# Attention of a hybrid decoder trunk: one stream of score visits in place of one schedule per head pair

## The chip, the cores and the metric

The kernel runs on one core of a Trainium2 chip. The metric is the device time of one execution in microseconds (us). TensorE (PE in the rows) multiplies matrices, VectorE (DVE) and ScalarE (ACT) work on elements, GpSimd (POOL) and SyncE (SP) issue transfers. Each of them has its own queue of instructions.

## The reference, cut to what matters

Layer 0 of the trunk is differential attention over 512 positions and 16 heads, layer 1 a chunked spatial gating MLP. Each head has two score maps; the second one's probabilities are weighted by lambda and subtracted from the first's.

```python
def probs(qq, kk):
    s = jnp.einsum('bhqd,bhkd->bhqk', qq, kk).astype(jnp.float32) * scale + bias
    s = jnp.where(causal, s, -jnp.inf)
    return jax.nn.softmax(s, axis=-1)
a = probs(q_i[0], k1) - lam * probs(q_i[1], k2)
return jnp.einsum('bhqk,bhkd->bhqd', a.astype(v.dtype), v)
...
o = rms_norm(o, subln_g) * (1.0 - lam_init)
```

The outputs of the heads are gated, multiplied by the output projection and added to the residual stream.

## The kernel before, in words

Products are done in halves of a number: every weight and every activation is split into a high and a low part (`hi`, `lo`: one copy on ScalarE, one subtraction on VectorE), and three matmuls of 512 columns stand for one product. A chunk of weights is loaded by SyncE into `raw` tiles and split in four pieces, which `Chunk.tick` spreads over the matmuls of the chunk before it.

Attention is the stage from 203 to 517 us of the trace. Its work comes in these steps:

- `project_qk(p)` makes the queries and keys of head pair p: 32 units, each of three matmuls (L254 to L256), with two chunks of weights split beside them. The results are read out of PSUM by ScalarE (`qkh`, L504) and VectorE (`qkl`, L505).
- A `Group` is a visit: one or two blocks of 128 queries, of one head or of both heads of a pair, side by side in tiles of 512 columns. The causal mask leaves block i with (i + 1) x 128 keys. A pair has five groups: (one, 3); (one, 2) and (one, 0); (one, 1) and (two, 1); (two, 3); (two, 2) and (two, 0).
- `Group.scores` issues 6 or 12 matmuls (L694); VectorE adds the bias and finds the maximum (L704), ScalarE takes exponentials and their sums (L707), two or four of each; VectorE then divides and subtracts the second map (L711 to L715). The result is `e`.
- `Group.flip` transposes `e` on TensorE (`pa`, L721), and ScalarE copies it out (`at`, L723).
- `Group.values` multiplies it by the values (`po`, L732). The last one of a head calls `Head.normalise`: four squares with sums on ScalarE (L662), eleven small VectorE instructions for the root (L180 to L192), and a product `on` (L666).
- `Head.close` transposes `on` on TensorE (`pto`, L672), and VectorE gates it into `yT` (L673).

`attention_steps` lays the five groups of one pair out in ten slots: scores in slots 0 to 4, the flip of group t in slot t + 2, its values in slot t + 3, the close of head one in slot 6 and that of head two in slot 9. `interleave` runs a slot and then as many units of the filler as keep it even over the ten slots: 3 or 4. The filler is `project_qk` of the next pair, 32 units; pairs 7 and 8 share the last projection and 48 units of the output projection (`out_half`, L273 to L275), 40 units each. At the end of a pair the filler is drained, and the next pair begins with slot 0. So scores are issued in the first half of a pair, and none in the second half.

The order in the code is a priority, not the order of the queues: a planner that reckons with times of its own lays out the queue of each engine when the kernel is built. A step whose inputs aren't ready by its reckoning lets later ones pass. On the chip each queue then runs in the order laid out. The eight banks of PSUM come from one pool, taken in turn by whatever step asks.

Of the kernel before, what the change touches and what calls it, by code (L numbers as in the profile page):

```python
# [10 lines left out]
F32 = mybir.dt.float32  # L11
F32R = mybir.dt.float32r
# [4 lines left out]
P = 128  # L17
D = 1024
S = 512
BR = 2048  # L20
NH = 16
HALF = 64
NB = S // P
# [27 lines left out]
def build(ctx, tc, x, rel_bias, attn_norm, w_in, lq1, lk1, lq2, lk2, subln, w_out,  # L51
# [14 lines left out]
    def bank(name):  # L66
        return psum.tile([P, S], F32, tag="ps", name=name)
# [102 lines left out]
    make_identity(nc, ident)  # L170
    flip = const.tile([P, P], F32, name="flip")
    nc.vector.tensor_copy(flip, ident[:, ::-1])

    MAGIC = 1597463007.0 - 2.0 ** 22 - 2.0 ** 30
# [14 lines left out]
    def rsqrt(dst, ssum, n, scale):  # L189

        v = small.tile([P, n], F32, name=f"rv{n}")
        nc.vector.tensor_scalar(v, ssum, -0.5 * scale, -0.5 * EPS, ALU.mult, ALU.add)  # L192
        newton(dst, v, n)
# [56 lines left out]
    def proj_t(ps, w, c):  # L250

        cs = slice(c * P, (c + 1) * P)
        for k in range(KD):
            nc.tensor.matmul(ps, lhsT=w.hi[:, k, cs], rhs=hT[0][:, k, :], start=(k == 0), stop=False)  # L254
            nc.tensor.matmul(ps, lhsT=w.hi[:, k, cs], rhs=hT[1][:, k, :], start=False, stop=False)  # L255
            nc.tensor.matmul(ps, lhsT=w.lo[:, k, cs], rhs=hT[0][:, k, :], start=False, stop=(k == KD - 1))  # L256
            w.tick()
            yield

    def out_half(i0, m, store, cs=range(4), acc=None, finish=None):  # L260

        for c in cs:
            w = Chunk(i0 + c, 16)
            yh, yl = store(c)
            for i in range(4):
                k = 4 * c + i
                nc.scalar.copy(yh[:, i], yT[:, k, :])  # L267
                nc.vector.tensor_tensor(yl[:, i], yT[:, k, :], yh[:, i].bitcast(F32), ALU.subtract)  # L268
            for b in range(NB):
                bs = slice(b * P, (b + 1) * P)  # L270
                for j in range(4):
                    k = 4 * c + j
                    nc.tensor.matmul(acc[b], lhsT=yh[:, j, bs], rhs=w.hi[:, j, :], start=(k == 0), stop=False)  # L273
                    nc.tensor.matmul(acc[b], lhsT=yh[:, j, bs], rhs=w.lo[:, j, :], start=False, stop=False)  # L274
                    nc.tensor.matmul(acc[b], lhsT=yl[:, j, bs], rhs=w.hi[:, j, :], start=False, stop=(k == KB - 1))  # L275
                    w.tick()
                    yield
                if c == 3:
                    finish(b)

    def run(g):
        for _ in g:
            pass
# [17 lines left out]
    def product_n(ps, a, w, start):  # L301

        more = {} if start else {"skip_group_check": True}
        for i in range(2):
            rs = slice(i * P, (i + 1) * P)
            for k in range(4):
                nc.tensor.matmul(ps[i], lhsT=a[0][:, k, rs], rhs=w[0][:, k, :], start=(start and k == 0), stop=False, **more)
                nc.tensor.matmul(ps[i], lhsT=a[0][:, k, rs], rhs=w[1][:, k, :], start=False, stop=False, **more)
                last_mm[:] = [nc.tensor.matmul(ps[i], lhsT=a[1][:, k, rs], rhs=w[0][:, k, :], start=False,
                                               stop=(k == 3), **more)]  # L310
                yield
# [98 lines left out]
    def residual(r, m, acc):  # L410
        def finish(b):
            ms = slice(m * S, (m + 1) * S)
            add = nc.vector.tensor_tensor(xr[:, b, ms], acc[b], xr[:, b, ms], ALU.add)
            square(r, b, m)
            if m == 0:
                half_mean(r, b)
            return add
        return finish
# [72 lines left out]
    def project_qk(p):  # L491
        qk = []
        for which in range(2):
            w = Chunk(qk_at[p] + which, 16)
            for j in range(2):
                ps = bank("psqk")
                yield from proj_t(ps, w, j)
                th = att.tile([P, NB, P], F32R, tag="qkh", name="qkh", bufs=6)
                tl = att.tile([P, NB, P], F32R, tag="qkl", name="qkl", bufs=6)
                sc = HALF ** -0.5 if which == 0 else 1.0  # L500
                pr = ps.rearrange("p (b n) -> p b n", b=NB)
                if which == 0:
                    pr = pr[:, :, ::-1]
                nc.scalar.activation(th, pr, AF.Copy, scale=sc)  # L504
                nc.vector.scalar_tensor_tensor(tl, pr, sc, th.bitcast(F32), ALU.mult, ALU.subtract)  # L505
                qk.append((th, tl))
        QK[p] = qk
# [49 lines left out]
    for c in range(2):  # L557
        pt = bank("pt")
        sl = slice(c * (TLEN // 2), (c + 1) * (TLEN // 2))
# [71 lines left out]
    att = scope.__enter__()  # L631

    def fetch_values(g):
        V[g] = att.tile([P, 4, NB, P], F32, name="v")
        nc.gpsimd.dma_start(V[g].rearrange("p j b n -> p (j b n)"), vd[g])

    fetch_values(0)
    run(project_qk(0))

    nc.scalar.activation(le, ls, AF.Exp)  # L640
# [3 lines left out]
    class Head:  # L644
# [12 lines left out]

        def normalise(self):
            ssq = small.tile([P, NB], F32, name="ssq")
            self.on = att.tile([P, NB, P], F32, name="on", bufs=1)  # L660
            for ii in range(NB):
                nc.scalar.activation(self.on[:, ii, :], self.po[:, ii * P:(ii + 1) * P], AF.Square,  # L662
                                     accum_out=ssq[:, ii:ii + 1])
            rs = small.tile([P, NB], F32, name="rso")
            rsqrt(rs, ssq, NB, 1.0 / P)
            nc.vector.tensor_tensor(self.on, self.po.rearrange("p (b n) -> p b n", b=NB),  # L666
                                    rs.unsqueeze(2).broadcast_to([P, NB, P]), ALU.mult)
# [7 lines left out]
    class Group:  # L675
# [42 lines left out]
        def flip(self):  # L718
            pa = bank("pa")
            for c in range(0, self.width, P):  # L720
                nc.tensor.transpose(pa[:, c:c + P], self.e[0][:, c:c + P], ident)  # L721
            self.at = att.tile([P, S], F32, name="at", bufs=2)
            nc.scalar.copy(self.at[:, 0:self.width], pa[:, 0:self.width])  # L723

        def values(self):
# [9 lines left out]
                if hd.left == 0:  # L735
                    hd.normalise()

    def attention_steps(heads):

        one, two = heads  # L740
        groups = [Group((one, 3)), Group((one, 2), (one, 0)), Group((one, 1), (two, 1)), Group((two, 3)),
                  Group((two, 2), (two, 0))]
        slots = [[] for _ in range(len(groups) + 5)]
        for t, g in enumerate(groups):
            slots[t].append((2, g.scores))
            slots[t + 2].append((0, g.flip))
            slots[t + 3].append((1, g.values))
        slots[6].append((3, one.close))
        slots[9].append((3, two.close))
        return [[f for _, f in sorted(sl, key=lambda z: z[0])] for sl in slots]  # L750

    def interleave(slots, filler, units, drain=True):
        n = len(slots)
        done = 0
        for t, sl in enumerate(slots):
            for f in sl:
                f()
            want = units * (t + 1) // n
            while done < want:
                if next(filler, StopIteration) is StopIteration:  # L760
                    break
                done += 1
        if drain:
            run(filler)

    i0 = out_at
    acc = {}

    def last_units():
        yield from project_qk(NH // 2 - 1)  # L770
        for b in range(NB):
            acc[b] = bank(f"acc{b}")
        yield from out_half(i0, 0, hT_store, range(3), acc)

    rest = last_units()
    for p in range(1, NH // 2 + 1):
        steps = attention_steps([Head(2 * p - 2), Head(2 * p - 1)])
        if p % 2 and p < NH // 2 - 1:
            fetch_values(p // 2 + 1)
        if p < NH // 2 - 1:  # L780
            interleave(steps, project_qk(p), 32)
        else:
            interleave(steps, rest, 40, p == NH // 2)
    scope.__exit__(None, None, None)
    quarters = tc.tile_pool(name="quarters", bufs=1)
    qp = quarters.__enter__()
# [120 lines left out]
    for n in range(BR // D):  # L907
        for i in range(7):
# [7 lines left out]
            units = product_n(ps, a, w, i in (0, 1, 3))  # L916
# [48 lines left out]
    for b in range(NB):  # L965
        sl = slice(b * P, (b + 1) * P)
# [31 lines left out]
    for m in range(2):  # L998
        for gates in (True, False):
            n = VB + 2 * m + (not gates)  # L1000
# [49 lines left out]
    last = residual(2, 1, acc)  # L1050
# [41 lines left out]
```

## Time and profile before

| what | us |
|---|---|
| median of 3 runs (lowest, highest) | 935.14 (934.59, 936.24) |
| the profiled execution, its own time | 936.22 |
| its span, first to last instruction | 934.5 |
| TensorE busy in the span | 898.9 |
| VectorE busy | 649.0 |
| ScalarE busy | 474.5 |

The profile is of one execution. Its own time is 1.1 us over the median, and 1.7 us of it lie outside the span. Busy times of TensorE are modelled at their ends: a matmul of 512 columns shows some 390 ns, but the next one starts about 230 ns after it.

### The profile page before, as it was taken

How to read it: one execution, taken by the hardware profiler on the slowest of the kernel's cores; microseconds unless marked ns; L12 is line 12 of the kernel's file. 1: busy time of each engine (PE TensorE's matmuls, PEld its weight loads, DVE VectorE, ACT ScalarE, POOL GpSimd, SP SyncE). 2: the span in 40 equal slices, each digit the busy share in tenths (PEclk: the TensorE clock that was granted, in tenths of full speed). 3: DMA queues.
4: the chain of work that ended last, by engine and by line, in shares of the span. 5: the costliest groups of instructions: out<-in, count | busy, mean ns of one | idle time of the engine just before them, and what ended most of it. 6: DMA issues, size and time to landing. Idle time of an engine off the chain costs nothing.

```text
span 934.5 us, 14107 instructions
## 1 busy us (share of the span) xinstructions
PE 898.9 (96%) x5393; PEld 772.1 (83%) x5393; DVE 649.0 (69%) x1399; ACT 474.5 (51%) x1015; POOL 34.3 (4%) x52
## 2 busy tenths in 40 slices
PE   7999999999999999999999999999999999999996
PEld 5778999977777777777777887778899999998885
DVE  6936575367767777677778937885978777776634
ACT  7635465356446454464556614663645444455432
POOL 0000100000000000000000001100100000000000
PEclk9999999999999999999999999999999999999999
DMA  8547745552132223122212604456455654534202
GB/s 291 214 103 214 202 159 113 183 183 82 61 102 63 87 77 103 57 66 91 71 45 88 249 24 110 135 139 195 106 172 125 193 135 137 114 112 139 90 21 90
DMA packets 55828, 115.48 MB, mean 124 GB/s; under 512 B 3965, under 2 KB 20398, under 8 KB 52432
## 3 DMA queue, kind: packets, MB, share of 16 engines
q1 hardware_dynamic: 49120, 79.70, 25.3%
q0 software_dynamic: 5584, 33.56, 15.0%
q10 hardware_dynamic: 1056, 1.32, 0.4%
q8 instruction: 42, 0.69, 0.3%
q14 instruction: 26, 0.21, 0.1%
HBM read 89.36 MB, written 6.33 MB: 102 GB/s over the span
## 4 chain that ended last, share of the span: by engine, by line
PE 62%; DVE 23%; ACT 8%; DMA 4%; issue 3%; SPq 0%; ACTq 0%; POOLq 0%; DVEq 0%
PE px L319 15%; PE py L319 11%; PE acc L273 5%; PE acc L274 5%; PE acc L275 5%; ACT e L707 5%; DVE lo L130 4%; PE psv L480 3%; DMA quarter<-quarter 3%; DVE e L715 3%; PE psqk L254 2%; PE psqk L255 2%; PE psqk L256 2%; DVE e L704 2%; DVE e L714 2%
## 5 line engine op out<-in xcount | busy, mean ns | idle before, releaser
L374 DVE TENSOR_TENSOR lo<-quarter,hi 128x1024 fp32r<-128x1024 f32 x126 | 152.7, 1234 | 87.3 <-ACT hi L373 86.9
L373 ACT CAST hi<-quarter 128x1024 fp32r<-128x1024 f32 x126 | 128.8, 1047 | 125.9 <-DMA quarter<-quarter 40.8
L130 DVE TENSOR_TENSOR lo<-raw,hi 128x512 fp32r<-128x512 f32 x144 | 94.2, 684 | 37.4 <-ACT hi L129 37.2
L129 ACT CAST hi<-raw 128x512 fp32r<-128x512 f32 x144 | 81.5, 621 | 67.2 <-PE psqk L255 37.1
L254 PE MATMUL psqk<-hT,hi 128*128 128x512 f32 x256 | 107.1, 418 | 0.0
L707 ACT ACTIVATE e<-e,nm 128x384 f32<-128x384 f32 (+3 forms) x128 | 70.6, 553 | 67.7 <-DVE nm L704 67.6
L256 PE MATMUL psqk<-hT,lo 128*128 128x512 f32 x256 | 101.9, 398 | 0.0
L255 PE MATMUL psqk<-hT,hi 128*128 128x512 f32 x256 | 101.1, 395 | 0.0
L319 PE MATMUL py<-hT,hi 128*128 128x256 f32 x512 | 93.0, 283 | 0.0
L273 PE MATMUL acc<-hi,hT 128*128 128x512 f32 x224 | 88.1, 393 | 0.0
L275 PE MATMUL acc<-hi,hT 128*128 128x512 f32 x224 | 87.4, 390 | 0.0
L274 PE MATMUL acc<-lo,hT 128*128 128x512 f32 x224 | 87.3, 390 | 0.0
L319 PEld LDWEIGHTS py<-hT,hi 128*128 128x128 f32 x512 | 79.7, 192 | 0.0
L319 PE MATMUL py<-hT,lo 128*128 128x256 f32 x256 | 72.4, 283 | 0.0
L254 PEld LDWEIGHTS psqk<-hT,hi 128*128 128x128 f32 x256 | 49.0, 191 | 15.4 <-issue 5.1
L704 DVE CUSTOM_DVE_ANT_0 e<-pss,bias 128x384 f32<-128x384 f32 (+3 forms) x128 | 55.6, 484 | 3.0 <-PE pss L694 2.9
L256 PEld LDWEIGHTS psqk<-hT,lo 128*128 128x128 f32 x256 | 48.7, 190 | 10.8
L255 PEld LDWEIGHTS psqk<-hT,hi 128*128 128x128 f32 x256 | 49.0, 191 | 8.7
L268 DVE TENSOR_TENSOR hT<-yT,hT 128x512 fp32r<-128x512 f32 x56 | 37.4, 688 | 25.6 <-PE acc L274 17.2
L267 ACT CAST hT<-yT 128x512 fp32r<-128x512 f32 x56 | 33.1, 621 | 38.0 <-PE acc L274 28.0
L273 PEld LDWEIGHTS acc<-hi,hT 128*128 128x128 f32 x224 | 42.1, 188 | 9.4 <-issue 0.7
L275 PEld LDWEIGHTS acc<-hi,hT 128*128 128x128 f32 x224 | 42.1, 188 | 9.0
(218 smaller groups left out, 2033.4 us busy)
## 6 DMA issues: line engine op xcount, KB each, us to landing
quarter<-in_sgu_w_in SPq DMA_DIRECT2D x48, 512.0 KB, 5.0
raw<-in_attn_w_in SPq DMA_DIRECT2D x38, 512.0 KB, 4.5
quarter<-quarter POOLq DMA_DIRECT2D x18, 1024.0 KB, 7.2
quarter<-in_attn_w_in SPq DMA_DIRECT2D x24, 512.0 KB, 4.8
raw<-in_attn_w_out SPq DMA_DIRECT2D x16, 512.0 KB, 4.3
raw<-in_sgu_w_out SPq DMA_DIRECT2D x16, 512.0 KB, 4.2
vd<-yT POOLq DMA_DIRECT2D x4, 1024.0 KB, 6.0
v<-vd POOLq DMA_DIRECT2D x4, 1024.0 KB, 5.0
```

The source lines that it names most:

```text
L129: nc.scalar.copy(hi[:, sl], raw)
L130: nc.vector.tensor_tensor(lo[:, sl], raw, hi[:, sl].bitcast(F32), ALU.subtract)
L254: nc.tensor.matmul(ps, lhsT=w.hi[:, k, cs], rhs=hT[0][:, k, :], start=(k == 0), stop=False)
L255: nc.tensor.matmul(ps, lhsT=w.hi[:, k, cs], rhs=hT[1][:, k, :], start=False, stop=False)
L256: nc.tensor.matmul(ps, lhsT=w.lo[:, k, cs], rhs=hT[0][:, k, :], start=False, stop=(k == KD - 1))
L273: nc.tensor.matmul(acc[b], lhsT=yh[:, j, bs], rhs=w.hi[:, j, :], start=(k == 0), stop=False)
L274: nc.tensor.matmul(acc[b], lhsT=yh[:, j, bs], rhs=w.lo[:, j, :], start=False, stop=False)
L275: nc.tensor.matmul(acc[b], lhsT=yl[:, j, bs], rhs=w.hi[:, j, :], start=False, stop=(k == KB - 1))
L319: nc.tensor.matmul(ps[f // 2][:, f % 2 * H:(f % 2 + 1) * H], lhsT=w[x][:, k, f * P:(f + 1) * P], rhs=a[y][:, k, :], start=clear, stop=(k = ...
L373: nc.scalar.copy(hi[:, sl], raw[:, sl])
L374: nc.vector.tensor_tensor(lo[:, sl], raw[:, sl], hi[:, sl].bitcast(F32), ALU.subtract)
L707: nc.scalar.activation(e[f][:, cs], e[f][:, cs], AF.Exp, scale=-1.0, bias=nm[:, col], accum_out=l[:, col])
```

## The change: what it does

The five visits of all eight pairs become one line of 40. Slot s issues the scores of visit s first, then two units of filler, the flip of visit s - 2, two more units, the values of the same visit, one unit, a close if one is due, and the rest of the units. A pair has five slots with 6 or 7 units each instead of ten with 3 or 4. Head one is closed in the first slot of the next pair and head two in its third, each one slot after its last values. The last pair has the 48 units of the output projection as filler and four more slots. Four kinds of tiles get more buffers: `qkh` and `qkl` 8 for 6, `on` 2 for 1, `at` 3 for 2.

```diff
-                th = att.tile([P, NB, P], F32R, tag="qkh", name="qkh", bufs=6)
-                tl = att.tile([P, NB, P], F32R, tag="qkl", name="qkl", bufs=6)
+                th = att.tile([P, NB, P], F32R, tag="qkh", name="qkh", bufs=8)
+                tl = att.tile([P, NB, P], F32R, tag="qkl", name="qkl", bufs=8)
...
-            self.on = att.tile([P, NB, P], F32, name="on", bufs=1)
+            self.on = att.tile([P, NB, P], F32, name="on", bufs=2)
...
-            self.at = att.tile([P, S], F32, name="at", bufs=2)
+            self.at = att.tile([P, S], F32, name="at", bufs=3)
...
-    def attention_steps(heads):
...
-        slots = [[] for _ in range(len(groups) + 5)]
-        for t, g in enumerate(groups):
-            slots[t].append((2, g.scores))
-            slots[t + 2].append((0, g.flip))
-            slots[t + 3].append((1, g.values))
-        slots[6].append((3, one.close))
-        slots[9].append((3, two.close))
-        return [[f for _, f in sorted(sl, key=lambda z: z[0])] for sl in slots]
-
-    def interleave(slots, filler, units, drain=True):
-        n = len(slots)
-        done = 0
-        for t, sl in enumerate(slots):
-            for f in sl:
-                f()
-            want = units * (t + 1) // n
-            while done < want:
...
-    def last_units():
-        yield from project_qk(NH // 2 - 1)
+    def out_units():
         for b in range(NB):
             acc[b] = bank(f"acc{b}")
         yield from out_half(i0, 0, hT_store, range(3), acc)
 
-    rest = last_units()
-    for p in range(1, NH // 2 + 1):
-        steps = attention_steps([Head(2 * p - 2), Head(2 * p - 1)])
-        if p % 2 and p < NH // 2 - 1:
-            fetch_values(p // 2 + 1)
-        if p < NH // 2 - 1:
-            interleave(steps, project_qk(p), 32)
-        else:
-            interleave(steps, rest, 40, p == NH // 2)
+    PAIRS, VISITS, LAG = NH // 2, 5, 2
+    line, heads = [], {}
+
+    def visits(p):
+        one, two = (Head(2 * p + i) for i in range(2))
+        heads[p] = one, two
+        return [Group((one, 3)), Group((one, 2), (one, 0)), Group((one, 1), (two, 1)), Group((two, 3)),
+                Group((two, 2), (two, 0))]
+
+    def slot(s, filler, units):
+
+        todo = []
+        if s < PAIRS * VISITS:
+            if s % VISITS == 0:
+                line.extend(visits(s // VISITS))
+            todo.append((0, line[s].scores))
+        if 0 <= s - LAG < len(line):
+            todo.append((2, line[s - LAG].flip))
+            todo.append((4, line[s - LAG].values))
+        for i, ready in enumerate((2, 4)):
+            p, r = divmod(s - LAG - ready - 1, VISITS)
+            if r == 0 and 0 <= p < PAIRS:
+                todo.append((5, heads[p][i].close))
+        done = 0
+        for at, f in todo:
+            while done < min(at, units) and next(filler, StopIteration) is not StopIteration:
+                done += 1
+            f()
+        while done < units and next(filler, StopIteration) is not StopIteration:
+            done += 1
+
+    tail = out_units()
+    for p in range(PAIRS):
+        if p % 2 == 0 and p < PAIRS - 2:
+            fetch_values(p // 2 + 1)
+        last = p == PAIRS - 1
+        filler = tail if last else project_qk(p + 1)
+        for r in range(VISITS + (LAG + 2 if last else 0)):
+            slot(p * VISITS + r, filler, 6 + (r in (1, 3)))
+        run(filler)
```

## Rows read from the trace of the kernel before

**Rows 1.** The page's first part: busy us, share of the span, instructions.

```profile
PE 898.9 (96%) x5393; PEld 772.1 (83%) x5393; DVE 649.0 (69%) x1399; ACT 474.5 (51%) x1015; POOL 34.3 (4%) x52
```

**Rows 2.** Busy time by stretch (PE, PEld, DVE, ACT, POOL; PEclk): attention, one pair of it.

```profile
203.20:517.50 314.30, 297.96 (x1733) 238.62 (x1732) 232.24 (x783) 170.50 (x537) 8.61 (x16) 0.99 0.24 76
241.40:280.90 39.50, 37.33 (x213) 29.85 (x212) 27.98 (x96) 20.03 (x66) 1.61 (x3) 0.96 0.29 94
```

**Rows 3.** Who waited for whom, 203.2 to 517.5 us: total, times, longest.

```profile
DVE r L711 <- ACT e L707: 34.9, 32, 1.3
...
DVE lo L130 <- ACT hi L129: 16.0, 7, 4.1
PE pto L672 <- DVE on L666: 13.9, 12, 2.1
DVE rv L192 <- ACT on L662: 11.1, 8, 1.7
DVE yT L673 <- PE pto L672: 10.3, 14, 1.0
...
PE pa L721 <- DVE e L715: 2.1, 6, 1.0
```

**Rows 4.** TensorE in order of time, the close of a head one.

```profile
262.07 1.06 PE L732 MATMUL po<-v,at 128*128 128x128 f32 x8
262.89 0.48 PE L254 MATMUL psqk<-hT,hi 128*128 128x512 f32 x1
...
268.22 0.39 PE L256 MATMUL psqk<-hT,lo 128*128 128x512 f32 x1
270.56 0.63 PE L672 MATMUL pto<-flip,on 128*128 128x128 f32 x4 [1.95 <-DVE on L666]
```

**Rows 5.** Busy time by stretch: a pair's crowded part, then its rest.

```profile
282.60:309.90 27.30, 25.28 (x158) 20.27 (x156) 22.23 (x80) 16.50 (x53) 1.07 (x2) 1.00 0.27 80
309.90:321.00 11.10, 10.76 (x56) 8.41 (x57) 5.78 (x19) 3.66 (x13) 0.00 (x0) 1.00 0.13 41
```

**Rows 6.** All engines in order of time, an uncrowded normalise (the last one).

```profile
511.60 0.47 PE L273 MATMUL acc<-hi,hT 128*128 128x512 f32 x1
...
515.30 0.69 DVE L666 TENSOR_TENSOR on<-po,rso 128x512 f32<-128x512 f32 x1
```

**Rows 7.** TensorE in order of time, the close of a head two.

```profile
316.33 0.30 PE L672 MATMUL pto<-flip,on 128*128 128x128 f32 x1 [0.18 <-DVE on L666]
```

**Rows 8.** All engines in order of time: units, scores, a crowded flip.

```profile
239.96 0.39 PE L254 MATMUL psqk<-hT,hi 128*128 128x512 f32 x1
...
240.65 0.39 PE L254 MATMUL psqk<-hT,hi 128*128 128x512 f32 x1
...
241.43 0.50 PE L694 MATMUL pss<-qkh 64*128 64x512 f32 x2
...
242.32 0.50 PE L254 MATMUL psqk<-hT,hi 128*128 128x512 f32 x1
...
247.80 0.60 PE L721 MATMUL pa<-ident,e 128*128 128x128 f32 x4
248.15 0.62 ACT L707 ACTIVATE e<-e,nm 128x384 f32<-128x384 f32 x1 [2.73 <-DVE nm L704]
...
248.33 0.39 PE L694 MATMUL pss<-qkh 64*128 64x256 f32 x2
...
250.14 0.56 ACT L723 COPY at<-pa 128x512 f32<-128x512 f32 x1
```

**Rows 9.** All engines in order of time, a flip that finds ScalarE nearly free.

```profile
505.35 0.60 PE L721 MATMUL pa<-ident,e 128*128 128x128 f32 x4
...
506.07 0.58 ACT L723 COPY at<-pa 128x512 f32<-128x512 f32 x1
```

**Rows 10.** GpSimd in order of time: a load of a bias, one of values.

```profile
262.31 0.54 POOL L655 DMA_DIRECT2D bias<-tb  x1 [8.78 <-DVE nm L704]
272.59 0.53 POOL L635 DMA_DIRECT2D v<-vd  x1 [9.74 <-PE po L732]
```

More of the change, by code (lines that the diff above doesn't have):

```diff
@@ L736, in values @@
                     hd.normalise()
-    def attention_steps(heads):
-        one, two = heads
-        groups = [Group((one, 3)), Group((one, 2), (one, 0)), Group((one, 1), (two, 1)), Group((two, 3)),
-                  Group((two, 2), (two, 0))]
-        slots = [[] for _ in range(len(groups) + 5)]
-        for t, g in enumerate(groups):
-            slots[t].append((2, g.scores))
-            slots[t + 2].append((0, g.flip))
-            slots[t + 3].append((1, g.values))
-        slots[6].append((3, one.close))
-        slots[9].append((3, two.close))
-        return [[f for _, f in sorted(sl, key=lambda z: z[0])] for sl in slots]
-    def interleave(slots, filler, units, drain=True):
-        n = len(slots)
-        done = 0
-        for t, sl in enumerate(slots):
-            for f in sl:
-                f()
-            want = units * (t + 1) // n
-            while done < want:
[L760 to L764, printed above, removed]
     i0 = out_at
     acc = {}
-    def last_units():
-        yield from project_qk(NH // 2 - 1)
+    def out_units():
         for b in range(NB):
```

## The prediction

> **What bounds the kernel now.** I read the page's first part, then the stage by stretches, then who waited for whom, then single closes in order of time. TensorE is busy for 96% of the span [rows 1], so only its idle time and the time it runs at a lower clock are to be had. Attention lasts 314.3 us, of which TensorE is busy for 298.0 [rows 2]: 16.3 us idle. The waits name nearly all of it: 13.9 us in which the transposes of a close (`pto`) wait for the normalised head (`on`), and 2.1 us in which a flip (`pa`) waits for `e` [rows 3]. The reader should see there that larger waits (VectorE's 34.9 us for exponentials) belong to engines that aren't the bound.
>
> A close shows the form of it. The last values of a head one end at about 262.9, TensorE is through with its units at 268.5, the transposes begin at 270.56, 1.95 us idle [rows 4]. The chain from those values to `on` took 7.5 us. An uncrowded one, the last of the stage, takes 515.99 - 511.60 = 4.4 us [rows 6]. The 3.1 us between them are crowding: in the first 27.3 us of a pair, where all its scores are, VectorE is busy for 22.2 us (81%), in the next 11.1 us for 5.8 (52%) [rows 5]; TensorE idles 2.0 us in the first and 0.3 in the second. A close of a head two, in the empty half, waits only 0.18 us [rows 7].
>
> The clock belongs to it. In one of the pairs the granted clock is 0.96 of full, which is a part of the stretch at the lower of its two levels, 1.2 for 2.4 GHz [rows 2]; in full-speed time that is 0.04 x 39.5 = 1.6 us. There are two such pairs, the others stand at 1.00, and the stage as a whole at 0.99: 3.2 us.
>
> **What the change removes.** Nothing computed changes: the same matmuls, copies and transfers. What can go is 13.9 (closes) + 2.1 (flips) + 3.2 (clock, if the idle time before it is what lowered it) = 19.2 us. To see how much of it goes I lay out a slot. A unit takes 240.65 - 239.96 = 0.69 us, scores 242.32 - 241.43 = 0.89 us [rows 8]; a flip 248.33 - 247.80 = 0.53 us [rows 8], values 262.89 - 262.07 = 0.82 us [rows 4].
>
> Scores to flip: was two slots less what stands between, 247.80 - 241.43 = 6.4 us [rows 8]. It becomes two whole slots and two units. A slot is 6.4 units x 0.69 + 0.89 + 0.5 + 0.8 = 6.6 us, so 13.2 + 1.4 = 14.6 us. That covers the longest flip wait (1.0 us) [rows 3] many times: -2.1 us, no bound needed above nothing.
>
> Values to close: 2 or 3 units left in the slot, then scores, a flip, values and 5 units: 7 x 0.69 + 0.89 + 0.5 + 0.8 = 7.0 us, one unit more for a head two. Uncrowded the chain takes 4.4 us, crowded 7.5: a wait of 0 to 0.5 us for each of 16 closes, 0 to 8 us together. VectorE will be as crowded as in [rows 5] all along, 232.2 us of work [rows 2] in 314.3 - 19.2 = 295.1 us, 79%. I charge the eight heads that have the shorter distance with a wait like that of [rows 7]: 8 x 0.18 = 1.4 us.
>
> **What it adds.** Flip to values shrinks most. They were a slot apart; now two units lie between, so values come 0.5 + 1.4 = 1.9 us after the flip's first transpose. Between them ScalarE must copy `at`. Where its queue is nearly free the copy ends 506.65 - 505.35 = 1.3 us after that transpose [rows 9]: no wait. In a crowded pair it ends 250.70 - 247.80 = 2.9 us after it, because four exponentials stand ahead (first at 248.15, copy at 250.14) [rows 8]: 1.0 us late. So the new wait is 0 to 1.0 us per visit, 0 to 40 us over 40 visits, and what is queued behind it on TensorE is all filler and the next scores. In the order of the code the values stand 4 x 0.69 + 0.53 = 3.3 us after the slot's scores; four exponentials and the copy take 250.70 - 248.15 = 2.55 us [rows 8], so the copy is in time if the first exponential begins within 0.74 us of the scores, and each tenth of a microsecond later costs 4 us over 40 visits. But the queues needn't have that order. The code asks for the values of a later group (L635) before any bias of the next pair, and the trace has the bias of 262.31 ahead of the values of 272.59 [rows 10]: what isn't ready by the planner's reckoning is passed by. So where the copy is late by its reckoning, matmuls of the filler will go ahead of the values, and what remains is the error of the reckoning. The nearest row for this error on a short, uncrowded chain is 0.18 us [rows 7]; the crowded 1.95 us [rows 4] is of a chain of some twenty instructions behind a saturated VectorE. I take the first for every visit: 0.18 us x 40 = 7.2 us.
>
> One page speaks against this edit. [Rows 8] show a copy that waited for four exponentials though its input was there. The Trainium skill, page "PSUM — Partial Sum Buffer", section "Engine vs sequencer instructions", says that ScalarE's queue is strictly first in, first out and that matmuls start and complete in program order: nothing repairs a bad order at run time. The trace agrees, in the copy at 250.14. By that rule alone, with the exponentials of the same slot always ahead, the sum would be that of the second rival below, about 956 us; by the row of an uncrowded wait it is the forecast.
>
> The end: the last pair's 48 units run out six units (4.1 us) after the last values, against a chain of 4.4 us [rows 6]: 0.3 us. Buffers (`qkh`, `qkl`, `on`, `at`) cost nothing in time; without them the longer distances would turn into waits for a free tile. PSUM: slots in steady state ask for at most eight banks (two for projections, two for scores, one flip, two `po`, one close), so I charge nothing; four go to the output projection in the last pair, as before. The loads of a bias keep their lead of more than two slots; SyncE's loads follow the units, whose number is the same.
>
> **The sum.** -19.2 + 7.2 + 1.4 + 0.3 = -10.3 us against the profiled execution's 936.2 us (span 934.5 and 1.7 around it), which gives 925.9 us. That execution is 1.1 us above the median of 935.1, so I forecast **924.8 us**.
>
> **The rivals.**
> *Everything is covered.* The copies and closes find their slack, only the 0.3 us of the end come back: 935.1 - 19.2 + 0.3 = 916.2 us. For it: all scores spread evenly, and the planner moves filler into the gaps. Against it: 79% on VectorE.
> *The copy takes over from the close (slower).* Each visit's values wait for `at` behind the exponentials of their own slot, 1.0 us as in [rows 8]: 935.1 - 19.2 + 40 = 955.9 us. It cancels the gain from 19.2 / 40 = 0.48 us per visit on. For it: 2.9 us in a crowded pair, against the 1.9 that the layout leaves. Against it: the copy could go early, since the planner is free to put it ahead of exponentials that aren't ready, or the values later.
> *VectorE's crowding spreads.* If TensorE idles everywhere as in the crowded part, 27.30 us for 25.28 of work [rows 5], the 295.1 us become 318.7: 4.4 us more than now, 939.5 us. For it: VectorE's share would be that of the crowded part in every slot, and its waits for exponentials (34.9 us) [rows 3] come back with every visit: 232.2 + 34.9 + 16.0 + 11.1 + 10.3 = 304.5 us, above TensorE's 295.1, if no other work fills them. Against it: the last three of those come for the most part from the thin half, where VectorE had nothing else to do.
> *The layout does not matter.* The planner lets filler pass whatever isn't ready, so that the waits measure its error and not the distance in the code; then the closes stay as late as they are: 935 us, within 2 us. Against it: a head two, in the thin half, waits 0.18 us by the same planner.
>
> **Chances.** Forecast with small new waits 0.58 (its own range 917 to 932: from new waits of a few hundredths to 0.4 us a visit, short of the 0.48 us that cancel the gain: 935.1 - 19.2 + 16 + 0.3); everything covered 0.14; the copy 0.10; crowding 0.08; no effect 0.10. A measurement of this kernel tells apart some 0.2%, 1.9 us. Faster 0.58 + 0.14 + 0.01 = 0.73, same 0.08, slower 0.10 + 0.08 + 0.01 = 0.19. For the range I leave out the copy's case and the upper half of the crowding: 914 to 938 us.
>
> **What the profile after would show.** If I am right: the wait of `pto` for `on` under 3 us in total, no pair of the stage under a clock of 1.00, `pa` waiting for nothing, a new wait of `po` for `at` of about 7 us in many small pieces, attention some 303 us long, and VectorE's 649 us unchanged. I am wrong if `po` waits for `at` by more than 0.48 us at a time, if `pto` still waits 1 us or more for `on`, or if scores (`pss`) wait for a bank of PSUM.

## The result, and the profile after

The change made the kernel faster: 922.12 us (921.33 to 922.37) against 935.69 us (934.59 to 937.31) for the kernel before, measured beside it; the ratio is 0.9842, 95% interval 0.9813 to 0.9872. Forecast were 924.8 us and a range of 914 to 938. The profiled execution took 921.33 us, its span 919.6.

The page's first part of the kernel after: busy us, share of the span, instructions.

```profile
span 919.6 us, 14089 instructions
...
PE 898.9 (98%) x5393; PEld 765.2 (83%) x5393; DVE 648.2 (70%) x1399; ACT 476.2 (52%) x1015; POOL 34.9 (4%) x52
```

TensorE is busy for the same 898.9 us as in [rows 1], in a span 14.9 us shorter. VectorE and ScalarE do the same work too. To see where the time went, I take a stretch with the same work in every kernel: from the first scores to the first transposes of layer 1's norm, so that it holds attention and the rest of the output projection, however these are mixed. The next two blocks are busy time by stretch (length, then TensorE, weight loads, VectorE, ScalarE, GpSimd, then TensorE's granted clock), first of the kernel before, then of the kernel after.

```profile
203.20:574.00 370.80, 354.46 (x1979) 284.85 (x1979) 267.57 (x845) 194.23 (x583) 9.49 (x17) 0.99 0.27 84
```

```profile
202.90:560.90 358.00, 354.31 (x1979) 277.68 (x1979) 266.66 (x845) 195.91 (x583) 9.48 (x17) 1.00 0.28 87
...
279.80:316.30 36.50, 36.08 (x216) 27.99 (x214) 27.86 (x97) 20.24 (x65) 1.61 (x3) 1.00 0.33 101
```

The stretch is 12.8 us shorter. TensorE's idle time in it fell from 16.3 to 3.7 us. The pair shown takes 36.5 us; that of [rows 2] took 39.5, 1.6 of them by the lower clock. The clock is now 1.00. Yet TensorE is busy as long as before, although the 3.2 us of lower clock are gone: the same 1979 matmuls show 3.1 us more. The waits tell why. Who waited for whom on the kernel after, 202.9 to 508.4 us (total, times, longest):

```profile
DVE r L711 <- ACT e L707: 31.7, 31, 1.5
...
PEld po L732 <- ACT at L723: 15.6, 37, 1.1
...
DVE rv L192 <- ACT on L662: 12.0, 14, 3.8
...
PE po L732 <- ACT at L723: 3.2, 7, 0.7
...
PE pto L672 <- ACT hi L129: 0.2, 1, 0.2
```

Set this against [rows 3]. The 13.9 us of closes waiting for `on` are gone, and so is every wait of a flip for `e`. A new one has come, as forecast: the values (`po`) wait for the copy (`at`). TensorE is seen idle for 3.2 us of it; the weight loads of those matmuls wait 15.6 us in 37 pieces. The runs below show that a part of this waiting stands in the trace as busy time of TensorE.

The longer waits of `po` sit in one place of a pair, the third slot. All engines of the kernel after, in order of time:

```profile
283.28 1.15 PE L732 MATMUL po<-v,at 128*128 128x128 f32 x8
...
285.64 0.17 DVE L192 TENSOR_SCALAR rv<-ssq 128x4 f32<-128x4 f32 x1 [0.51 <-ACT on L662]
...
285.84 0.17 DVE L180 TENSOR_SCALAR ry<-rv 128x4 int32<-128x4 int32 x1
...
287.14 0.28 PE L694 MATMUL pss<-qkh,qkl 64*128 64x256 f32 x2
...
287.81 0.69 DVE L666 TENSOR_TENSOR on<-po,rso 128x512 f32<-128x512 f32 x1
288.42 0.41 DVE L704 CUSTOM_DVE_ANT_0 e<-pss,bias 128x256 f32<-128x256 f32 x1
...
288.83 0.60 PE L721 MATMUL pa<-ident,e 128*128 128x128 f32 x4
288.88 0.51 ACT L707 ACTIVATE e<-e,nm 128x256 f32<-128x256 f32 x1 [3.27 <-DVE nm L704]
...
290.87 0.56 ACT L723 COPY at<-pa 128x512 f32<-128x512 f32 x1
...
291.48 0.71 PE L732 MATMUL po<-v,at 128*128 128x128 f32 x4 [0.42 <-ACT at L723]
```

Read it as one chain. The last values of head two end at 284.2, and its normalise takes VectorE from 285.64 to 288.5: eleven small instructions, each reading the result of the one before, and the product `on`. The scores of the next visit end at about 287.4, but their maxima are behind the normalise in VectorE's queue and begin at 288.42. The four exponentials follow, and the copy of the earlier visit's transposes, ready since about 289.4, is behind them on ScalarE: it runs at 290.87, and the values at 291.48.

### The profile page after: what moved, and what is told of

Read it like the earlier page. It is cut to its first block, busy times and chain, and to the rows that moved or that the text cites. A ratio compares the mean times of both kernels' runs of the same rounds, so it can differ in the third digit from the quotient of the medians.

```text
span 919.6 us, 14089 instructions
## 1 busy us (share of the span) xinstructions
PE 898.9 (98%) x5393; PEld 765.2 (83%) x5393; DVE 648.2 (70%) x1399; ACT 476.2 (52%) x1015; POOL 34.9 (4%) x52
## 4 chain that ended last, share of the span: by engine, by line
PE 82%; DVE 9%; ACT 5%; DMA 2%; issue 1%; ACTq 0%; DVEq 0%; POOLq 0%
PE px L319 15%; PE py L319 11%; PE psqk L254 5%; PE acc L273 5%; PE acc L275 5%; PE acc L274 5%; PE psqk L256 5%; PE psqk L255 5%; PE po L732 4%; PE psv L480 4%; PE pss L694 3%; ACT e L707 2%; PE px L307 2%; PE px L308 2%; PE px L309 2%; PE psy L980 2%
## 5 line engine op out<-in xcount | busy, mean ns | idle before, releaser
L254 PE MATMUL psqk<-hT,hi 128*128 128x512 f32 x256 | 110.3, 431 | 0.0
L255 PE MATMUL psqk<-hT,hi 128*128 128x512 f32 x256 | 100.7, 393 | 0.0
L256 PEld LDWEIGHTS psqk<-hT,lo 128*128 128x128 f32 x256 | 48.0, 188 | 10.7
L732 PEld LDWEIGHTS po<-v,at 128*128 128x128 f32 x320 | 38.9, 191 | 15.9 <-ACT at L723 15.6
L275 PEld LDWEIGHTS acc<-hi,hT 128*128 128x128 f32 x224 | 42.1, 188 | 9.0
```

## The experiments

Each kernel was run beside the kernel before on the same chip; the ratios are to that. The first four go by the forecast's main terms.

**Buffers alone.**

```diff
-                th = att.tile([P, NB, P], F32R, tag="qkh", name="qkh", bufs=6)
-                tl = att.tile([P, NB, P], F32R, tag="qkl", name="qkl", bufs=6)
+                th = att.tile([P, NB, P], F32R, tag="qkh", name="qkh", bufs=8)
+                tl = att.tile([P, NB, P], F32R, tag="qkl", name="qkl", bufs=8)
...
-            self.on = att.tile([P, NB, P], F32, name="on", bufs=1)
+            self.on = att.tile([P, NB, P], F32, name="on", bufs=2)
...
-            self.at = att.tile([P, S], F32, name="at", bufs=2)
+            self.at = att.tile([P, S], F32, name="at", bufs=3)
```

> The kernel before with the change's buffers alone (qkh and qkl 8, on 2, at 3). If the distance in the layout made the gain (my theory): no change, 935.7 us within 1.9, and pto still waits some 14 us for on. If the waits of before were a shortage of tiles: most of the gain, some 922 us.

Measured: 936.63 us, ratio 0.9993 (0.9977 to 1.0009). The queues of all five engines come out the same as before, instruction for instruction, and so does the wait of closes (13.1 us). The waits of before weren't a shortage of tiles.

**One close one slot later, in the kernel before.**

```diff
-        slots[6].append((3, one.close))
+        slots[7].append((3, one.close))
```

> The kernel before with one line changed: head one is closed in slot 7 instead of 6, 2.9 us later (three units and the values of the last group). If the late close is the cost and distance cures it: some 13 us of the 13.9 of idle time go, and the 3.2 us of lower clock with them, 919 to 922 us. If the crowding of VectorE in the first half is what has to go (an even stream is needed): the wait moves to the next step, and no more than 3 us are won, 932 us or more.

Measured: 926.8 us, ratio 0.9899 (0.9881 to 0.9918), between the two. Waits of this run (total, times, longest):

```profile
PE pto L672 <- DVE on L666: 6.2, 12, 1.1
PE pa L721 <- DVE e L715: 2.2, 6, 1.0
```

The wait was halved and did not move to another step. I had reckoned 2.9 us per close; a wait of 1.95 us became 0.96, so the slot gave 1.0. TensorE in order of time, first before, then in this run:

```profile
265.49 1.06 PE L732 MATMUL po<-v,at 128*128 128x128 f32 x8
```

```profile
265.84 1.06 PE L732 MATMUL po<-v,at 128*128 128x128 f32 x8
...
268.81 1.05 PE L732 MATMUL po<-v,at 128*128 128x128 f32 x8
270.83 0.66 PE L672 MATMUL pto<-flip,on 128*128 128x128 f32 x4 [0.96 <-DVE on L666]
```

In the code of before, the close of slot 6 stands right behind the values of 265.49 and ahead of three units. In the queue these units, which end with the matmul of 268.22 in [rows 4], already stand ahead of it: the planner had let them pass. The later slot moved the close behind one more step only, the values of the last group (268.81), 0.8 us.

**Values behind the fifth unit, in the kernel after.**

```diff
-            todo.append((4, line[s - LAG].values))
+            todo.append((5, line[s - LAG].values))
```

> The kernel after with the values behind the fifth unit of a slot instead of the fourth, so that the copy has 0.69 us more. If the waits of po for at are a cost of the layout: the 3.2 us of TensorE's idle time and most of the 15.6 us for which weight loads of po wait go, 917 to 920 us. If these waits are the planner's own (it puts the values where the copy is just ready, wherever they stand): 922.1 within 1 us.

Measured: 918.37 us, ratio 0.9805 (0.9781 to 0.983). The waits, TensorE's own and those of its weight loads for the copy:

```profile
PE pto L672 <- DVE on L666: 1.6, 7, 0.2
PE po L732 <- ACT at L723: 0.8, 2, 0.5
```

```profile
PEld po L732 <- ACT at L723: 1.7, 2, 0.9
```

One unit, 0.69 us, takes both waits for the copy away but for two in the slots of the last pair, and now the closes wait a little.

**Values behind the third unit.** The same line with 3.

> The kernel after with the values behind the third unit instead of the fourth, so that the copy has 0.69 us less. Strict order of the code: 40 times up to 0.69 us more of waiting, 940 us or more. If the planner lets filler pass the values: the waits grow little, some 922 to 926 us.

Measured: 930.79 us, ratio 0.9939 (0.9921 to 0.9956), between the two again. TensorE idles 10.7 us in 14 pieces, weight loads wait at each of the 40 visits:

```profile
PE po L732 <- ACT at L723: 10.7, 14, 1.4
```

```profile
PEld po L732 <- ACT at L723: 24.9, 40, 1.8
```

40 x 0.69 = 27.6 us earlier in the code cost 9 us: the planner lets filler pass, but not enough. So the wait does depend on the place that the code gives the values.

**The close two slots later, in the kernel before.**

```diff
-        slots[6].append((3, one.close))
+        slots[8].append((3, one.close))
-            self.on = att.tile([P, NB, P], F32, name="on", bufs=1)
+            self.on = att.tile([P, NB, P], F32, name="on", bufs=2)
```

> The kernel before with head one closed in slot 8, two slots later than it was, and two buffers for on; one slot later won some 10 us and left 6.2 us of waits of pto for on. If the distance alone decides: these 6 us go too, 920 to 921 us, and nothing of the stream is needed for it. If the planner always sets the close where on is just ready by its reckoning: the wait stays, 925 to 927 us.

Measured: 920.23 us, ratio 0.983 (0.9811 to 0.9849). By waits and by the stretch with the same work:

```profile
PE pa L721 <- DVE e L715: 2.2, 6, 1.0
PE pto L672 <- DVE on L666: 1.2, 6, 0.2
```

```profile
203.60:557.00 353.40, 350.05 (x1980) 282.86 (x1980) 265.81 (x845) 194.40 (x583) 9.49 (x17) 1.00 0.28 89
```

Two lines in the old schedule give as much as the whole stream; the two intervals overlap. The later close alone is enough for a gain of this size, and in the stretch it is 4.6 us ahead of the stream (353.4 us to 358.0). The waits of flips, which the stream removed, stay at 2.2 us here.

**Values at five and the close at the end of its slot.**

```diff
-            todo.append((4, line[s - LAG].values))
+            todo.append((5, line[s - LAG].values))
-                todo.append((5, heads[p][i].close))
+                todo.append((7, heads[p][i].close))
```

> The kernel after with the values behind the fifth unit and the close at the end of its slot, two units later than it was. Values at five alone gave 918.4 us and left 1.6 us of idle time before closes. Distance theory: 916 to 917 us, TensorE waiting for under 1.5 us in the stage. If something else sets the rest: 918.4 within 1 us.

Measured: 916.14 us, ratio 0.9782 (0.9762 to 0.9802), faster than both kernels.

```profile
203.20:554.20 351.00, 350.01 (x1979) 281.39 (x1979) 262.84 (x845) 195.30 (x583) 9.49 (x17) 1.00 0.28 89
```

TensorE idles 1.0 us in the stretch, and its busy time is 4.3 us less than in the kernel after, for the same matmuls. The matmuls of the values (count, then busy us and mean ns), in the kernel after and in this run:

```profile
L732 PE MATMUL po<-v,at 128*128 128x128 f32 x320 | 45.6, 285 | 3.5 <-ACT at L723 3.2
```

```profile
L732 PE MATMUL po<-v,at 128*128 128x128 f32 x320 | 42.3, 275 | 0.8 <-ACT at L723 0.8
```

3.3 of the 4.3 us lie in these 320 matmuls, whose weight loads waited for the copy for 15.6 us in the one kernel and 1.7 in the other. So the 3.1 us more were, for the most part, late weight loads, booked as busy.

**Flip right behind the scores, close at the end.**

```diff
-            todo.append((2, line[s - LAG].flip))
+            todo.append((0, line[s - LAG].flip))
-                todo.append((5, heads[p][i].close))
+                todo.append((7, heads[p][i].close))
```

> The kernel after with the flip right behind the scores (two units earlier), the values still behind the fourth unit and the close at the end: the copy has 2.8 us, and the filler is cut into two stretches per slot instead of three, some 90 instead of 135. The traces gave 3.1 us more TensorE time for 62 more stretches, 0.05 us each. If a stretch costs that: 2 us less than the run with values at five and close at seven, 914 to 915 us. If stretches cost nothing: the same as that run, 916 to 917 us.

Measured: 917.65 us, ratio 0.9803 (0.9782 to 0.9824), not told apart from the run before it. The stretch is 0.6 us shorter, with 1.7 us less busy time and one wait of 1.7 us at a flip:

```profile
203.80:554.20 350.40, 348.33 (x1980) 280.74 (x1980) 266.07 (x845) 196.70 (x583) 9.49 (x17) 1.00 0.28 89
```

```profile
PE pa L721 <- DVE yT L673: 1.7, 1, 1.7
```

My idea that each break of the filler costs 0.05 us was made for the 3.1 us, which the run before explains for the most part otherwise. 1.7 us for some 39 breaks less would be 0.04 us each. Against that price, the old schedule with the close two slots later has 42 breaks less than the run before (79 to 121) and is busy for the same 350.0 us; so it stays open.

**One slot from scores to flip.**

```diff
-    PAIRS, VISITS, LAG = NH // 2, 5, 2
+    PAIRS, VISITS, LAG = NH // 2, 5, 1
```

> The kernel after with one slot from scores to flip instead of two (6.6 + 1.4 = 8.0 us; before it was 6.4 us, with waits of up to 1.0 us). If flips have slack to spare: 922.1 within 2 us, with pa waiting for e less than 2 us. If the two slots are what the stream lives on: flips wait at every visit, 40 times up to 0.5 us, 930 us or more.

Measured: 941.71 us, ratio 1.0062 (1.0043 to 1.0082), slower than before. But not by the flips, which wait for nothing:

```profile
PE po L732 <- ACT at L723: 15.3, 16, 1.4
```

All of its idle time is the copy's, in 16 pieces, two per pair. In order of time, one of them:

```profile
287.87 0.69 DVE L666 TENSOR_TENSOR on<-po,rso 128x512 f32<-128x512 f32 x1
...
288.48 0.55 DVE L704 CUSTOM_DVE_ANT_0 e<-pss,bias 128x384 f32<-128x384 f32 x1
...
289.07 0.62 ACT L707 ACTIVATE e<-e,nm 128x384 f32<-128x384 f32 x1 [3.41 <-DVE nm L704]
...
291.05 0.56 ACT L723 COPY at<-pa 128x512 f32<-128x512 f32 x1
```

```profile
291.67 1.16 PE L732 MATMUL po<-v,at 128*128 128x128 f32 x8 [1.41 <-ACT at L723]
```

It is the chain of the kernel after. With one slot the normalise of both heads stands ahead of a visit with four exponentials; with two slots that of head one stands ahead of a visit with only two. The waits and the busy time in the stretch make 14.7 us of the difference to the kernel after (372.7 us to 358.0); the profiled execution also took 7.2 us more behind the stretch (365.9 to 358.7), which the copy doesn't explain.

**The same with a shorter normalise.** One round of Newton's iteration in a head's root instead of three: six small VectorE instructions less, and a coarser root.

```diff
-        for it in range(3):
+        for it in range(3 - rounds, 3):
...
-            rsqrt(rs, ssq, NB, 1.0 / P)
+            rsqrt(rs, ssq, NB, 1.0 / P, 1)
```

> The run with one slot from scores to flip (941.7 us), with one round of Newton's iteration in a head's normalise instead of three: six small VectorE instructions less, some 1.2 us of the chain, and a coarser root. There TensorE waited 15.3 us in 16 pieces for the copy, each behind a normalise. If the normalise holds VectorE's queue in front of the maxima of the next visit and so makes the exponentials and the copy late: nearly all of it goes, 924 to 928 us. If the waits are the planner's error on any layout: the values move up with it, 936 us or more.

Measured: 928.3 us, ratio 0.9898 (0.9877 to 0.992).

```profile
PE po L732 <- ACT at L723: 3.3, 10, 0.9
```

1.2 us less in the chain takes 12 of 15.3 us of idle time and 1.6% of the whole. Nothing in this edit touches exponentials, copies or values, and TensorE's queue is that of the run before up to 469 us, with 12 places of 5393 changed behind it; so the normalise in VectorE's queue is what makes the copy late.

**A shorter normalise in the kernel before.** The same edit, in the kernel before.

> The kernel before with one round instead of three in a head's normalise (a coarser root). If the close waits for the length of that chain: 7 or 8 waits of 2 us shrink by 1.2 us, 8 to 10 us, and the lower clock behind them may go as well, 923 to 928 us. If the planner sets the close by its reckoning and the wait is its error: the close moves up with the shorter chain and the wait stays, 933 us or more.

Measured: 928.6 us, ratio 0.9903 (0.9887 to 0.992), and still

```profile
PE pto L672 <- DVE on L666: 9.8, 7, 1.8
```

```profile
203.50:565.20 361.70, 349.88 (x1979) 282.52 (x1979) 253.23 (x749) 194.63 (x583) 9.51 (x17) 1.00 0.27 86
```

```profile
269.09 0.63 PE L672 MATMUL pto<-flip,on 128*128 128x128 f32 x4 [1.69 <-DVE on L666]
```

Both readings hold in part. The time fell by some 9 us, but only 4.1 of them are waits of closes (13.9 to 9.8); 3.2 are the lower clock, which no pair of the first six shows here, and the rest is mostly busy time. A close of a head one still waits up to 1.8 us: five matmuls of filler now stand between the values ahead of it and the close, where there were nine, so the planner set it earlier as the chain grew shorter.

**The old buffers in the kernel after.** The buffers of the first experiment, the other way.

> The kernel after with the buffers of before (qkh and qkl 6, on 1, at 2). My prediction held that the stream needs the new ones: waits for a free tile at each head or visit, some 925 to 935 us. If tiles come free in time as they were: 922.1 within 2 us.

Measured: 924.96 us, ratio 0.9868 (0.9849 to 0.9886). The queues of all engines are the same, instruction for instruction, as those of the kernel after, and the stretch takes 358.4 us against 358.0:

```profile
203.20:561.60 358.40, 354.22 (x1980) 277.72 (x1980) 266.82 (x845) 195.81 (x583) 9.49 (x17) 1.00 0.28 87
```

So the buffers do nothing that shows, and the 0.3% between the two ratios is what two measurements of the same queues may differ by; the two intervals overlap.

## Why the prediction was right

**What could go, 19.2 us.** It went: idle time in closes 13.9 to 0.2 us, in flips 2.1 to nothing, and no stretch of attention shows the lower clock. That the clock followed from the idle time is borne out, not proven: it is back at 1.00 in the stretch of every kernel shown above whose closes wait less, and two pairs are at 0.96 again in the run with the buffers alone, where TensorE waited as before. But the wait doesn't decide alone. In the kernel before, five closes of a head one waited 1.95 to 2.07 us; the clock fell to its lower level behind two of them, those at 270.56 and 386.80, and behind the longest, at 348.52, it did not:

```profile
271.00:276.00 5.00, 5.00 (x21) 4.18 (x20) 2.22 (x8) 1.74 (x9) 0.53 (x1) 0.66 0.61 200
...
348.00:353.00 5.00, 4.48 (x26) 3.97 (x27) 2.65 (x10) 1.74 (x9) 0.53 (x1) 1.00 0.58 171
```

**The new wait for the copy, 7.2 us.** The size was right, and its form was not, so that the agreement of the size is in part luck. I charged 0.18 us to each of 40 visits, as what remains when the planner lets filler pass a late copy. In the queue of the kernel after, the last pair aside, it did so for one visit of a pair only, in its third slot, and there by one matmul (seven between the flip of 288.83 and the values of 291.48, where the code has six). Measured are 3.2 us of idle time and 3.1 us of late weight loads, 6.3 us; moving the values by one unit, with the close out of the way, took 7.0 us off the stretch. The longer pieces, six of about 0.4 us like that at 291.48, sit in the third slot of a pair, where the normalise of head two holds up the maxima, those the exponentials, and those the copy. The second rival named exponentials ahead of the copy, but not what makes them late. The Trainium skill, page "PSUM — Partial Sum Buffer", section "Engine vs sequencer instructions", calls the queues of VectorE and ScalarE strictly first in, first out. The trace agrees twice in that chain, at 288.42 and at 290.87.

**Closes and the end, 1.7 us.** 0.2 us were measured. A close of a head one in the kernel after, all engines:

```profile
269.39 1.16 PE L732 MATMUL po<-v,at 128*128 128x128 f32 x8
270.31 0.47 PE L254 MATMUL psqk<-hT,hi 128*128 128x512 f32 x1
...
273.97 0.68 DVE L704 CUSTOM_DVE_ANT_0 e<-pss,bias 128x512 f32<-128x512 f32 x1
...
275.41 0.57 ACT L723 COPY at<-pa 128x512 f32<-128x512 f32 x1
...
275.94 0.68 DVE L666 TENSOR_TENSOR on<-po,rso 128x512 f32<-128x512 f32 x1
...
277.73 0.60 PE L672 MATMUL pto<-flip,on 128*128 128x128 f32 x4
```

The close stands 7.4 us behind its last values, 7.0 were reckoned, and the chain takes 6.3 us, between the 4.4 and the 7.5 of the sum. That of a head two takes 4.3 us, though no slot is empty any more. The margin of a head one is thus about 1 us: with values at five its chain took 7.4 us, and the closes waited 1.6 us in all.

**The sum.** -12.8 us in the stretch against -10.3: 1.5 us by closes and the end, 0.9 by the copy. The medians are 13.6 us apart, 0.8 more than that, which I can't place. The program behind the stretch varies by more than this between two executions: 358.7 us in the kernel after, 360.7 in the run with the old buffers, whose queues are the same.

**What failed.** The sentence that the buffers are needed for the longer distances: without them the queues are the same. The sentence that flips gain from two slots is right in that their waits went, yet one slot would have done as much for them. The second slot is worth 2% of the time; the 14.7 us of it that lie in the stretch come nearly all by way of the copy. That this is because it moves the normalise of head one ahead of a visit with two exponentials is read from the order of the rows, not tested by itself; the rows also show that visit's maxima between the small instructions of the normalise (273.97) and its copy in time (275.41). And the rival in which the layout doesn't matter, since the planner passes what isn't ready: it does matter, by 9 us for one unit. One sign of being wrong came true, too: `po` waited for `at` by more than 0.48 us at a time, once, by 0.7 us in the last pair; the other pieces are shorter. Attention was to be some 303 us long (the sum gives 304.0) and took 305.5.

**What the change is worth by itself.** The stream and a close two slots later in the old schedule come out alike, 0.9842 and 0.983. What the rewrite does beyond that, flips without waits and an even load, was paid back by the wait for the copy, in the stretch with more than it gave (358.0 us to 353.4); behind the stretch the profiled execution of the old schedule took 3.0 us more, where two executions of the same queues differ by 2.0. With one unit more for the copy and a close at the end of its slot it gives 0.9782.

## What to carry to other kernels

A consumer's place in the queue must leave room for all that stands ahead of its producer, on every queue of the chain: here eleven small instructions on VectorE delayed a copy on ScalarE that does not read their result. Before a schedule is rewritten, move the one step that waits: two lines gave what forty did. Look at waits of weight loads beside TensorE's idle time, since part of the waiting is booked as busy.

## What the runs showed of the hardware that I had not expected

The same 1979 matmuls at full clock show 354.3 us of busy time with 15.6 us of late weight loads and 350.0 us with 1.7: some 30% of the loads' waiting is in the busy time. The share isn't fixed: with the values at three, 24.9 us of waiting go with 355.8 us. And a chain of eleven VectorE instructions on four columns, some 0.16 us each, takes 0.20 us per step when each reads the last one's result (from 285.64 on). What comes behind it in the queue, the maxima of 288.42, did not start in the gaps; only where the planner had laid other instructions between the steps, as at 273.97, was the time used.
